# A hybrid layer in one kernel: a pool shared by two projection stages with early loads, gate rows on GpSimd's queue, and x normalised in pairs of tiles

## The chip, the core and the metric

The kernel runs on one core of a Trainium2 chip. The metric is the device time of one execution in microseconds, and a kernel's time is the median of its runs.

## What is computed

One layer of a streaming encoder on x, 2048 tokens by 1024 channels in float32. The stream is normalised, and one projection w_in makes the columns of four mixers: S5 (a diagonal complex state space model), RWKV-7, stick-breaking attention and an mLSTM with a matrix memory. Their outputs, 256 channels each, are concatenated and projected; then follows a gated feed-forward with a causal convolution. Of the reference, the parts that the change touches:

```python
def layer_norm(x, g, b):
    xf = x.astype(jnp.float32)
    mu = jnp.mean(xf, -1, keepdims=True)
    var = jnp.mean(jnp.square(xf - mu), -1, keepdims=True)
    return ((xf - mu) * lax.rsqrt(var + LN_EPS) * g + b).astype(x.dtype)
...
    b = jnp.cumsum(chunks(jax.nn.log_sigmoid(fg)), axis=-1)
    b_last = b[..., -1]
    g = b_last[..., None] - b + ig
    m_loc = jnp.max(g, -1)
...
        m_new = jnp.maximum(bl + m_st, ml)
        s_old = jnp.exp(bl + m_st - m_new)
        s_new = jnp.exp(ml - m_new)
```

The first function is the input normalisation. The rest is the mLSTM's gate arithmetic: the input gates ig and forget gates fg, four rows (heads) by 2048 tokens, give decays and a running maximum for every token.

## The kernel before

Every large product is made in three matmuls: both factors are split into a high and a low part (`wch`, `wcl` for weights, `hTh`, `hTl` for tokens), and high by high, low by high and high by low are summed. A projection of 128 columns over a block of 512 tokens is 8 pieces of the inner dimension times 3, 24 matmuls of 128x512. The instructions of each engine run in the order in which a scheduler puts them from the program; each engine, and each queue of transfers, is in order. A tile pool gives out its buffers again when the last use of a tile is over, and a pool that is opened later may get the memory of a closed one, and then waits for that one's last uses.

The stages, by the time at which TensorE works at them: P, the projections of S5 and RWKV (0 to about 363 us), with S5's set-up and its four blocks between them; Q, the projections of the attention and the mLSTM, begins behind S5's last block and then fills gaps in R (RWKV, to about 1045 us); S (attention) with X (mLSTM) to about 1425 us; the output projection O to about 1605; the feed-forward U and D to the end.

*Stage P* (`phase_p`) has four blocks of 512 tokens. `layer_in(tb)` loads four tiles of x (128 tokens each), takes mean and variance on VectorE (`bn_stats`, `bn_aggr`), the reciprocal root on GpSimd (`rsqrt`), -mean*rs and the normalised tile on VectorE (lines 290 and 291). TensorE transposes the tiles (line 298), VectorE makes u = p*g+b (line 300), ScalarE rounds u to the high part (line 301), and VectorE and GpSimd in turn subtract it to get the low part (line 302). Both parts go to the scratch tensor `hT_d`, from which stage Q reads its tokens again. `layer_in` of the next block is called at the end of a block.

*Stage Q* (`phase_q`) opens its own pools after those of P are closed. It loads a block's tokens in eight transfers, then its weights, and splits them (`load_w`: ScalarE rounds, GpSimd subtracts). Its small constants come by GpSimd's queue.

*Stage X* (`phase_x`) starts with the gate rows: r_f and r_ig are loaded as 64 rows of 128 from `gt_d`, which Q wrote; r_lf, the log of the sigmoid, goes to `ml_lf_d`; then four steps, one for each block of 512 tokens, load two rows of gates, scan them with VectorE (`mrow`, line 666) and store the result (`ml_m_d`, `ml_p_d`). The scans' results are read back as r_mr and r_mp, from which come the rows that are stored to `ml_rowd` and loaded again as `mb` and `wib`. All these transfers are issued by SP's queue, in which the loads of attention stand too: `kst` (keys), `qdh` and `qdl` (queries in two parts), `v` and `sb_dv` (values). In the attention, TensorE makes scores (`a`, from `kst` and `qdh`), ScalarE turns them into `sb_stay`, VectorE scans them (`af`, line 507), TensorE transposes the scan (`b`) and multiplies it with the values (`c`).

## Time and profile before

| | before |
|---|---|
| median of 3 runs | 2933.1 us (2932.53 to 2935.2) |
| the profiled execution, its own time | 2929.18 us |
| span in the profile | 2927.5 us |
| mean granted clock of TensorE | 0.967 of full |
| TensorE (PE) busy | 2744.1 us, 94% |
| VectorE (DVE) busy | 1944.7 us, 66% |
| ScalarE (ACT) busy | 1249.4 us, 43% |
| GpSimd (POOL) busy | 753.8 us, 26% |

A profile follows one execution. Its times count from the start of the span. PE is TensorE's matmuls, PEld its loading of weights, SP an engine that only issues transfers; a q behind a name is that engine's queue. A row of a timeline gives start, duration, engine, line, operation, what is written and what is read, the tile's size and, in brackets, how long the engine was idle before and whose work ended that. "Full clock" is 2.4 GHz, and 0.50 of it 1.2 GHz.

### The profile page before, as it was taken

To read this page: it belongs to the slowest core of one execution; us is meant where nothing else is said; L and a number is where in the kernel's file an instruction comes from. 1 tells how busy PE (TensorE), PEld (TensorE's weight loads), DVE (VectorE), ACT (ScalarE), POOL (GpSimd) and SP (SyncE) were. 2 spreads that over 40 slices of the span, in tenths; PEclk is the share of its full clock that TensorE was granted. 3 is DMA by queue.
4 is the path that set the end of the run, shared out by engine and by line. 5 is a ranking of instruction groups with operands and counts; after the bars stand their busy time and mean duration, and the time that the engine had idled before them with its cause. 6 is when DMAs were issued, how large, how long until landed. Compare 5 with 4: busy or idle time off the path is not lost. (4 is left out here: it accounts for less than half of the span.)

```text
span 2927.5 us, 42242 instructions
## 1 busy us (share of the span) xinstructions
PE 2744.1 (94%) x15515; PEld 2168.4 (74%) x15515; DVE 1944.7 (66%) x3109; ACT 1249.4 (43%) x2103; POOL 753.8 (26%) x800
## 2 busy tenths in 40 slices
...
GB/s 182 130 207 218 155 188 136 171 122 174 117 138 121 58 176 158 133 54 69 224 241 204 208 154 160 151 166 260 229 197 198 195 194 195 246 265 189 198 160 123
DMA packets 495775, 502.51 MB, mean 172 GB/s; under 512 B 105088, under 2 KB 383488, under 8 KB 492752
## 3 DMA queue, kind: packets, MB, share of 16 engines
...
q14 instruction: 85, 0.70, 0.1%
q10 hardware_dynamic: 1744, 0.14, 0.0%
...
## 5 line engine op out<-in xcount | busy, mean ns | idle before, releaser
L143 PE MATMUL u_ps<-bh,wh 128*128 128x512 f32 x1232 | 482.7, 392 | 5.1 <-ACT hr L189 1.8
L144 PE MATMUL u_ps<-bl,wh 128*128 128x512 f32 x1232 | 481.9, 391 | 0.3 <-DVE bl L1483 0.3
L145 PE MATMUL u_ps<-bh,wl 128*128 128x512 f32 x1232 | 480.3, 390 | 0.0
L1513 ACT CAST wh<-wr 128x512 fp32r<-128x512 f32 x308 | 191.1, 622 | 412.6 <-PE u_ps L144 326.0
L135 POOL TENSOR_TENSOR wcl<-wraw,wch 128x512 fp32r<-128x512 f32 (+1 forms) x152 | 249.1, 1649 | 448.2 <-ACT wch L132 419.7
L1514 DVE TENSOR_TENSOR wl<-wr,wh 128x512 fp32r<-128x512 f32 x308 | 210.9, 687 | 164.1 <-ACT wh L1513 163.8
L143 PEld LDWEIGHTS u_ps<-bh,wh 128*128 128x128 f32 x1232 | 231.5, 188 | 58.4 <-ACT g L1615 2.1
L145 PEld LDWEIGHTS u_ps<-bh,wl 128*128 128x128 f32 x1232 | 231.5, 188 | 50.3
L144 PEld LDWEIGHTS u_ps<-bl,wh 128*128 128x128 f32 x1232 | 231.7, 188 | 48.7 <-DVE bl L1483 0.6
L1571 POOL DMA_DIRECT2D ad_d<-cv x132 | 95.5, 726 | 639.0 <-DVE cv L1557 607.7
L132 ACT CAST wch<-wraw 128x512 fp32r<-128x512 f32 (+1 forms) x152 | 110.2, 731 | 263.8 <-PE m L144 146.7
L143 PE MATMUL m<-hT,wch 128*128 128x512 f32 x448 | 189.2, 424 | 3.7 <-ACT wch L132 2.8
L145 PE MATMUL m<-hT,wcl 128*128 128x512 f32 x448 | 184.9, 413 | 2.6 <-POOL wcl L135 2.6
L144 PE MATMUL m<-hT,wch 128*128 128x512 f32 x448 | 184.2, 412 | 0.0
L106 DVE TENSOR_TENSOR da<-da 128x1024 fp32r<-128x1024 f32 (+1 forms) x84 | 104.8, 1280 | 65.1 <-ACT da L103 64.9
L103 ACT CAST da<-da 128x1024 fp32r<-128x1024 f32 (+1 forms) x84 | 79.5, 976 | 149.5 <-DMA da<-ad_d 149.0
L507 DVE TENSOR_TENSOR_SCAN af<-sb_stay,af,sb_zero 128x513 f32<-128x513 f32 x96 | 120.4, 1274 | 28.8 <-ACT sb_stay L502 26.7
L144 PE MATMUL m<-hTl,wch 128*128 128x512 f32 x320 | 130.6, 408 | 7.5 <-POOL hTl L302 6.6
L143 PE MATMUL m<-hTh,wch 128*128 128x512 f32 x320 | 127.4, 404 | 6.9 <-DVE rw_halo L336 6.9
L145 PE MATMUL m<-hTh,wcl 128*128 128x512 f32 x320 | 127.3, 398 | 0.0
L502 ACT ACTIVATE sb_stay<-a 128x512 f32<-128x512 f32 (+3 forms) x160 | 86.0, 539 | 91.7 <-PE a L498 43.1
L1553 DVE SCALAR_TENSOR_TENSOR cv<-u,ffn_cw,cv 128x1024 f32<-128x1024 f32 x88 | 112.7, 1281 | 15.8 <-ACT cv L1551 15.7
...
## 6 DMA issues: line engine op xcount, KB each, us to landing
...
ad_d<-S POOLq DMA_DIRECT2D x176, 128.0 KB, 3.8
...
ad_d<-cv POOLq DMA_DIRECT2D x132, 128.0 KB, 2.8
```

Of the source, the lines that this page charges most:

```text
L106: nc.vector.tensor_tensor(lo, src, r32(hi), op=ALU.subtract)
L132: nc.scalar.copy(hi[:, kk, cs], raw)
L135: (lo_eng or nc.vector).tensor_tensor(lo[:, kk, cs], raw, r32(hi[:, kk, cs]), op=ALU.subtract)
L143: nc.tensor.matmul(ps, lh, rh, start=start and i == 0, stop=False, **kw)
L144: nc.tensor.matmul(ps, lh, rl, start=False, stop=False, **kw)
L145: nc.tensor.matmul(ps, ll, rh, start=False, stop=i == n - 1, **kw)
L502: nc.scalar.activation(r[:, ns], lgn, AF.Sigmoid, scale=-1.0)
L507: nc.vector.tensor_tensor_scan(af[:, back], r[:, back], zero.to_broadcast([128, n + 1]), p["af"][:, TB - p["n"]:TB - p["n"] + 1] if p else ...
L1513: nc.scalar.copy(h, r)
L1514: V(l, r, r32(h), op=ALU.subtract)
L1553: STT(cv, u[:, d:d + 1024], cw[:, f, d:d + 1], cv, op0=ALU.mult, op1=ALU.add)
L1571: nc.gpsimd.dma_start(K_.ad_d[i - 1, fb, c, :, j, :].rearrange("p (n c) -> p n c", c=128), t[:, 2 * c:2 * c + 2, :])
```

## The change

It does four things.

1. A new pool, `early`, holds the tiles of x, u, and the token blocks of every other block, and Q's token blocks and weights use the same buffers. It stays open from the start of P to the end of Q. `hT_d` becomes one tensor for each block, written in eight transfers.
2. `phase_q` is started inside P's last block, ahead of the third of its six last RWKV projections (`QAT`): it then loads its first token block and its first two weights. Its constants live in the kernel's constant pool and are loaded by SP's queue.
3. In `layer_in`, the reciprocal root is taken for two tiles at once; -mean*rs is a `tensor_scalar`; the normalised tile is made by ScalarE from block 1 on, and for the second tile of each pair in block 0; u is made by ScalarE from block 1 on, and the low parts there all by VectorE. x is requested ahead of the norm's gain and bias.
4. The 22 transfers of the gate rows go from SP's to GpSimd's queue.

```diff
...
         rs = pool.tile([128, 1], F32, tag="ln_rs", name="ln_rs")
         self.rsqrt(pool, rs, mv[:, 1:2], LN_EPS)
         nm = pool.tile([128, 1], F32, tag="ln_nm", name="ln_nm")
-        nc.vector.scalar_tensor_tensor(nm, mv[:, 0:1], -1.0, rs, op0=ALU.mult, op1=ALU.mult)
+        nc.vector.tensor_scalar(nm, mv[:, 0:1], rs, -1.0, op0=ALU.mult, op1=ALU.mult)
         nc.scalar.activation(t, t, AF.Identity, scale=rs, bias=nm)
...
     return cv
-def phase_p(K_, st, st5):
+def phase_p(K_, st, st5, early, ahead):
...
             q(nc).dma_start(t, src.rearrange("(f p) -> p f", p=128))
             return t
-        def layer_in(tb):
+        def xrows(tb):
             xs = []
             for i in range(4):
...
+                x = early.tile([128, D], F32, tag="x", bufs=4, name="x")
+                nc.sync.dma_start(x, a["x"][0, (tb * 4 + i) * 128:(tb * 4 + i) * 128 + 128, :])
                 xs.append(x)
-            hi = w.tile([128, KD, TB], F32R, tag="hTh", name="hTh")
-            lo = w.tile([128, KD, TB], F32R, tag="hTl", name="hTl")
+            return xs
+        def layer_in(tb, xs):
+            for j in range(0, 4, 2):
+                mv = w.tile([128, 2, 2], F32, tag="ln_mv", name="ln_mv")
+                for i in range(2):
+                    st = w.tile([128, 2, 6], F32, tag="ln_st", bufs=4, name="ln_st")
+                    for q in range(2):
+                        nc.vector.bn_stats(st[:, q, :], xs[j + i][:, q * 512:(q + 1) * 512])
+                    nc.vector.bn_aggr(mv[:, i], st)
+                ti = tb * 4 + j
+                K_.rsqrt(w, K_.lnst[:, ti:ti + 2, 1], mv[:, :, 1], LN_EPS)
+                for i in range(2):
+                    x, nm, rs = xs[j + i], K_.lnst[:, ti + i, 0:1], K_.lnst[:, ti + i, 1:2]
+                    TS(nm, mv[:, i, 0:1], rs, -1.0, op0=ALU.mult, op1=ALU.mult)
+                    if tb or i:
+                        nc.scalar.activation(x, x, AF.Identity, scale=rs, bias=nm)
+                    else:
+                        TS(x, x, mv[:, i, 0:1], rs, op0=ALU.subtract, op1=ALU.mult)
+            hs = [token_block((early, w)[tb % 2]) for _ in range(4)]
+            hT = [(h[:, k, :], l[:, k, :]) for h, l in hs for k in range(2)]
             for k in range(KD):
                 p = K_.psum("a", 2) if tb == 0 else K_.psum("c", 1)
                 for i in range(4):
                     nc.tensor.transpose(p[:, i * 128:(i + 1) * 128], xs[i][:, k * 128:(k + 1) * 128], K_.ident)
-                u = w.tile([128, TB], F32, tag="u", name="u")
-                TS(u, p, g[:, k:k + 1], b[:, k:k + 1], op0=ALU.mult, op1=ALU.add)
-                nc.scalar.copy(hi[:, k, :], u)
-                last = (nc.gpsimd if k % 2 else nc.vector).tensor_tensor(lo[:, k, :], u, r32(hi[:, k, :]),
-                                                                         op=ALU.subtract)
+                u = early.tile([128, TB], F32, tag="u", bufs=2, name="u")
+                if tb:
+                    nc.scalar.activation(u, p, AF.Identity, scale=g[:, k:k + 1], bias=b[:, k:k + 1])
+                else:
+                    TS(u, p, g[:, k:k + 1], b[:, k:k + 1], op0=ALU.mult, op1=ALU.add)
+                nc.scalar.copy(hT[k][0], u)
+                last = (nc.gpsimd if tb == 0 and k % 2 else nc.vector).tensor_tensor(hT[k][1], u, r32(hT[k][0]), op=ALU.subtract)
             K_.hold = last.ins
-            nc.sync.dma_start(K_.hT_d[tb, 0], r32(hi))
-            nc.sync.dma_start(K_.hT_d[tb, 1], r32(lo))
-            return [(hi[:, k, :], lo[:, k, :]) for k in range(KD)]
+            for q, t in enumerate(hs):
+                for i in range(2):
+                    nc.sync.dma_start(K_.hT_d[tb][i][:, 2 * q:2 * q + 2, :], r32(t[i]))
+            return hT
+        xs = xrows(0)
         g, b = chan("ln_in_g", a["ln_in_g"], KD, P1Q), chan("ln_in_b", a["ln_in_b"], KD, P1Q)
-        hT = layer_in(0)
+        hT = layer_in(0, xs)
         mu = chan("rw_mu", a["rw_mu"][0], 8, P2Q)
...
             nc.scalar.activation(xg, xg, AF.Sigmoid)
             nc.sync.dma_start(K_.rz_d[tb, 10], xg)
             for s in (2, 0, 4, 3, 1, 5):
+                if s == QAT and tb == K_.ntb - 1:
+                    ahead()
                 nc.sync.dma_start(K_.rz_d[tb, s], mixed(s))
-            hT = layer_in(tb + 1) if tb + 1 < K_.ntb else None
+            hT = layer_in(tb + 1, xrows(tb + 1)) if tb + 1 < K_.ntb else None
             if tb == FCB:
...
+def token_block(pool):
+    return [pool.tile([128, 2, TB], F32R, tag=n, bufs=4, name=n) for n in ("hTh", "hTl")]
+def phase_q(K_, st, early):
     tc, nc, a = K_.tc, K_.nc, K_.a
     w_in = a["w_in"][0]
     STT = nc.vector.scalar_tensor_tensor
-    c = st.enter_context(tc.tile_pool(name="qc", bufs=1, reuse_waits="tile", side="right"))
+    c = K_.const
+    def tokens(tb):
+        hT = []
+        for q in range(4):
+            hq = token_block(early)
+            for i in range(2):
+                HTQ(nc).dma_start(r32(hq[i]), K_.hT_d[tb][i][:, 2 * q:2 * q + 2, :])
+            hT += [(hq[0][:, k, :], hq[1][:, k, :]) for k in range(2)]
+        return hT
+    def weights(c0):
+        hi, lo = (early.tile([128, KD, 128], F32R, tag="x", bufs=4, name=n) for n in ("wch", "wcl"))
+        for k in range(0, KD, 4):
+            raw = early.tile([128, 4, 128], F32, tag="u", bufs=2, name="raw")
+            nc.sync.dma_start(raw, w_in.rearrange("(k p) n -> p k n", p=128)[:, k:k + 4, c0:c0 + 128])
+            nc.scalar.copy(hi[:, k:k + 4], raw)
+            nc.gpsimd.tensor_tensor(lo[:, k:k + 4], raw, r32(hi[:, k:k + 4]), op=ALU.subtract)
+        return hi, lo
+    hT, first = tokens(0), [weights(OFF_MLQ + i * 128) for i in range(2)]
+    yield
     w = st.enter_context(tc.tile_pool(name="qw", bufs=2, reuse_waits="tile", side="right"))
     cw = c.tile([128, 4, 4], F32, name="ml_cw")
     for j in range(4):
-        nc.gpsimd.dma_start(cw[:, :, j], a["ml_conv_w"][0, j].rearrange("(f p) -> p f", p=128))
+        nc.sync.dma_start(cw[:, :, j], a["ml_conv_w"][0, j].rearrange("(f p) -> p f", p=128))
...
     for tb in range(K_.ntb):
         tcs = slice(tb * TB, (tb + 1) * TB)
-        hT = []
-        for q in range(4):
-            hq = [w.tile([128, 2, TB], F32R, tag=f"hT{i}", bufs=4, name=f"hT{i}") for i in range(2)]
-            for i in range(2):
-                HTQ(nc).dma_start(r32(hq[i]), K_.hT_d[tb, i][:, 2 * q:2 * q + 2, :])
-            hT += [(hq[0][:, k, :], hq[1][:, k, :]) for k in range(2)]
+        if tb:
+            hT = tokens(tb)
         def cm(c0):
-            wt = load_w(K_, w, w_in, c0, 128, "wc", 2, rawpool=w, rtag="raw", rbufs=QRB, kpiece=4, eng=QENG, lo_eng=nc.gpsimd)
+            wt = first.pop(0) if first else weights(c0)
             p = K_.psum("mm", 3)
             proj_cm(K_, wt, hT, p)
             return p
...
     row = lambda n: c.tile([NG, L], F32, name="r_" + n)
     ig, f, lf, na, bb, gg, mr = (row(n) for n in ("ig", "f", "lf", "na", "b", "g", "mr"))
     mp, ml = c.tile([NG, 1], F32, name="r_mp"), c.tile([NG, 1], F32, name="r_ml")
-    nc.sync.dma_start(f, hc(K_.gt_d[4:8]))
-    nc.sync.dma_start(ig, hc(K_.gt_d[0:4]))
+    nc.gpsimd.dma_start(f, hc(K_.gt_d[4:8]))
+    nc.gpsimd.dma_start(ig, hc(K_.gt_d[0:4]))
     nc.vector.scalar_tensor_tensor(na, f, -1.0, f, op0=ALU.mult, op1=ALU.min)
...
     for tb in range(K_.ntb):
         cs = slice(tb * TB, (tb + 1) * TB)
         l4, i4 = (w.tile([128, TB], F32, tag=f"qw{n}", bufs=1, name="gates")[0:4] for n in range(2))
-        nc.sync.dma_start(l4, lf_d[:, cs])
-        nc.sync.dma_start(i4, K_.gt_d[0:4, cs])
+        nc.gpsimd.dma_start(l4, lf_d[:, cs])
+        nc.gpsimd.dma_start(i4, K_.gt_d[0:4, cs])
         if tb:
             nc.vector.tensor_copy(mrow[:, 0:1], mrow[:, TB:TB + 1])
         nc.vector.tensor_tensor_scan(mrow[:, 1:], l4, i4, mrow[:, 0:1], op0=ALU.add, op1=ALU.max)
-        nc.sync.dma_start(m_d[:, cs], mrow[:, 1:])
-        nc.sync.dma_start(p_d[:, tb * NCH:(tb + 1) * NCH], mrow[:, 0:TB:L])
-    nc.sync.dma_start(mr, hc(m_d))
-    nc.sync.dma_start(mp, p_d.rearrange("h c -> (h c)").unsqueeze(1))
+        nc.gpsimd.dma_start(m_d[:, cs], mrow[:, 1:])
+        nc.gpsimd.dma_start(p_d[:, tb * NCH:(tb + 1) * NCH], mrow[:, 0:TB:L])
+    nc.gpsimd.dma_start(mr, hc(m_d))
+    nc.gpsimd.dma_start(mp, p_d.rearrange("h c -> (h c)").unsqueeze(1))
...
     dr = lambda name, *sh: k.dram.tile(list(sh), F32, name=name)
     k.z5_d = dr("z5_d", k.ntb, 2, 128, S5J, S5N)
     k.y5_d = dr("y5_d", k.ntb, 128, 8, S5N)
-    k.hT_d = dr("hT_d", k.ntb, 2, 128, KD, TB)
+    k.hT_d = [dr(f"hT_d{tb}", 2, 128, KD, TB) for tb in range(k.ntb)]
...
-    left, right = ExitStack(), ExitStack()
+    left, right, right_p = ExitStack(), ExitStack(), ExitStack()
+    early = right.enter_context(tc.tile_pool(name="px", bufs=1, reuse_waits="tile", side="right"))
+    q = phase_q(k, right, early)
     s5 = none
     if "P" in parts:
-        for tb, _ in enumerate(phase_p(k, right, left)):
+        for tb, _ in enumerate(phase_p(k, right_p, left, early, lambda: next(q))):
             if tb == 0:
                 s5 = ahead(s5_main(k, left), S5HP)
             for _ in range(S5_IN_P[tb]):
                 next(s5, None)
-        right.close()
-    q = phase_q(k, right) if "Q" in parts else none
+        right_p.close()
...
 HTQ, ZQ, YQ, CQ = SY, SY, SY, SY
-QRB, QENG = 2, "act"
+QAT = 4
...
```

The lines of the changed program are numbered anew; the rows below carry the new numbers for the changed order.

On TensorE, at the seam between P and Q, the rows before are the last products of S5's fourth block (`b`, from the scans' result `Sx`) and the start of Q's first projection (`m1_3014`):

```order
L1379 MATMUL b_3201<-Sx1_2880,s5_CI_365 128x128
L1377 MATMUL b_3201<-U_2874,s5_MT_366 128x128
L1379 MATMUL b_3201<-Sx0_2879,s5_CR_364 128x128
L1379 MATMUL b_3201<-Sx1_2880,s5_CI_365 128x128
L143 MATMUL m1_3014<-hT0_2988,wch_3004 128x512
L144 MATMUL m1_3014<-hT1_2989,wch_3004 128x512
```


Of the change, at the same place. First the end of Q's second projection (`m2_3081`; the first, `m1_3043`, stands in front of it) and the first products of S5's fourth block (`b_3158`), with Q's third projection (`m0_3182`) between them:

```order
L144 MATMUL m2_3081<-hTl_2702,wch_2715 128x512
L145 MATMUL m2_3081<-hTh_2701,wcl_2716 128x512
L1416 MATMUL b_3158<-U_2932,s5_MT_376 128x128
L1418 MATMUL b_3158<-Sx0_2937,s5_CR_374 128x128
L1418 MATMUL b_3158<-Sx1_2938,s5_CI_375 128x128
L1416 MATMUL b_3158<-U_2932,s5_MT_376 128x128
L143 MATMUL m0_3182<-hTh_2689,wch_3172 128x512
L1418 MATMUL b_3158<-Sx0_2937,s5_CR_374 128x128
L144 MATMUL m0_3182<-hTl_2690,wch_3172 128x512
```


and, some 30 rows further, the end of the third projection, the first of the other products of that block (`b_3220`) and the matmuls of S5's output gate (`m1_3244`):

```order
L143 MATMUL m0_3182<-hTh_2701,wch_3172 128x512
L144 MATMUL m0_3182<-hTl_2702,wch_3172 128x512
L1418 MATMUL b_3220<-Sx0_2937,s5_CR_374 128x128
L145 MATMUL m0_3182<-hTh_2701,wcl_3173 128x512
L1434 MATMUL m1_3244<-yc_2992,s5_wglu_1115 128x512 x2
L1418 MATMUL b_3220<-Sx1_2938,s5_CI_375 128x128
L1416 MATMUL b_3220<-U_2932,s5_MT_376 128x128
```


Q's first projection came behind all products of S5's fourth block; now two projections come ahead of them and the third among them.

On SP's queue, in the middle of the attention, before: the last two steps of the gate rows, with the attention's loads between them.

```order
L667 DMA ml_m_d<-mrow 4x512
L668 DMA ml_p_d<-mrow 4x4x1
L662 DMA gates<-ml_lf_d 4x512
L663 DMA gates<-gt_d 4x512
L562 DMA qdh<-sk_d 64x2x512
L563 DMA qdl<-sk_d 64x2x512
L667 DMA ml_m_d<-mrow 4x512
L668 DMA ml_p_d<-mrow 4x4x1
L567 DMA v<-sv_d 128x2x256
L567 DMA sb_dv<-sv_d 128x2x256
L669 DMA r_mr<-ml_m_d 64x128
L670 DMA r_mp<-ml_p_d 64x1
```


Of the change, at the same place of the attention; `mb` and `wib` are the first loads that need the finished gate rows.

```order
L600 DMA kst<-sk_d 64x4x512
L601 DMA qdh<-sk_d 64x2x512
L602 DMA qdl<-sk_d 64x2x512
L600 DMA kst<-sk_d 64x4x512
L601 DMA qdh<-sk_d 64x2x512
L602 DMA qdl<-sk_d 64x2x512
L606 DMA v<-sv_d 128x2x256
L606 DMA sb_dv<-sv_d 128x2x256
L734 DMA mb<-ml_rowd 128x4x512
L740 DMA wib<-ml_rowd 64x2x512 x2
L606 DMA v<-sv_d 128x2x256
L606 DMA sb_dv<-sv_d 128x2x256
```


The loads of `kst`, `qdh`, `qdl` and the first values now stand ahead of everything that has to do with gate rows; the second pair of values stands behind `mb` and `wib`.

On GpSimd, of the change, the head of the gate rows (`ml_mask` is a constant of the mLSTM; its memory is that of one of Q's tiles, and it waits for the last matmuls of Q's last projection):

```order
L668 MEMSET ml_mask 128x128
L685 DMA r_f<-gt_d 64x128
L669 AFFINE_SELECT ml_mask<-ml_mask 128x128
L686 DMA r_ig<-gt_d 64x128
L691 DMA ml_lf_d<-r_lf 64x128
L701 DMA gates<-ml_lf_d 4x512
L702 DMA gates<-gt_d 4x512
L706 DMA ml_m_d<-mrow 4x512
L707 DMA ml_p_d<-mrow 4x4x1
L701 DMA gates<-ml_lf_d 4x512
```


None of these transfers stood on GpSimd before; all that stood there around this place was the two instructions on `ml_mask`.

## Rows read from the trace of the kernel before

**Rows 1.** The page, part 1: busy us (share) x instructions of each engine.

```profile
PE 2744.1 (94%) x15515; PEld 2168.4 (74%) x15515; DVE 1944.7 (66%) x3109; ACT 1249.4 (43%) x2103; POOL 753.8 (26%) x800
```

**Rows 2.** Timeline of PE, 0 to 60 us: start us, us, instruction [idle before <-releaser].

```profile
22.78 0.69 PE L298 MATMUL a<-ident,x 128*128 128x128 f32 x2 [5.55 <-DVE x L291]
...
58.33 0.47 PE L298 MATMUL c<-ident,x 128*128 128x128 f32 x1 [10.41 <-DVE x L291]
```

**Rows 3.** Waits of PE: waited for, us in total, times, longest us.

```profile
PE m L143 <- DVE rw_halo L336: 6.9, 1, 6.9
```

**Rows 4.** Timeline of PE, 363 to 400 us.

```profile
380.97 0.80 PE L1379 MATMUL b<-Sx,s_CR 128*128 128x128 f32 x2 [6.78 <-DVE Sx L1361]
...
387.31 0.77 PE L143 MATMUL m<-hT,wch 128*128 128x512 f32 x1
...
393.11 0.39 PE L145 MATMUL m<-hT,wcl 128*128 128x512 f32 x1
397.10 1.95 PE L1395 MATMUL m<-yc,s_wglu 128*128 128x512 f32 x4 [3.60 <-DVE ml_halo L259]
```

**Rows 5.** Timeline of PE, 1090 to 1150 us.

```profile
1136.02 0.66 PE L497 MATMUL a<-kst,qdh 128*128 128x128 f32 x2 [11.37 <-DMA qdh<-sk_d]
1137.28 0.44 PE L498 MATMUL a<-kst,qdl 128*128 128x128 f32 x1 [0.60 <-DMA qdl<-sk_d]
...
1142.41 0.36 PE L681 MATMUL m<-ident,r_ig 64*128 64x64 f32 x1 [0.98 <-ACT r_ig L675]
```

**Rows 6.** Stretches: length, busy (x) of five engines, PEclk, DMA share, GB/s.

```profile
40.00:60.00 20.00, 9.45 (x51) 7.07 (x49) 19.52 (x54) 6.07 (x15) 10.14 (x7) 0.76 0.60 227
360.00:380.00 20.00, 13.66 (x87) 10.93 (x85) 19.42 (x43) 7.84 (x10) 1.75 (x4) 0.95 0.63 181
380.00:400.00 20.00, 13.87 (x52) 10.49 (x52) 7.83 (x16) 5.62 (x9) 3.19 (x3) 0.79 0.63 202
1130.00:1145.00 15.00, 7.40 (x34) 5.37 (x34) 5.77 (x11) 4.87 (x10) 0.00 (x0) 0.50 0.59 151
```

**Rows 7.** Timeline of DVE, 5 to 30 us.

```profile
17.60 2.29 DVE L290 SCALAR_TENSOR_TENSOR lnst<-ln_mv,lnst 128x1 f32<-128x1 f32 x1 [1.00 <-POOL lnst L78]
19.81 2.91 DVE L291 TENSOR_SCALAR x<-x,ln_mv,lnst 128x1024 f32<-128x1024 f32 x1
```

**Rows 8.** Lines 291 to 302: count, ns min/median/max, first and last start, forms.

```profile
L291 DVE TENSOR_SCALAR x<-x,ln_mv,lnst x16: 799/806/2908, 10.2 to 272.4; 128x1024 f32<-128x1024 f32 x16
...
L300 DVE TENSOR_SCALAR u<-c,ln_in_g,ln_in_b x24: 780/800/811, 124.6 to 302.0; 128x512 f32<-128x512 f32 x24
...
L301 ACT CAST hTh<-u x32: 608/620/624, 24.1 to 302.8; 128x512 fp32r<-128x512 f32 x32
...
L302 DVE TENSOR_TENSOR hTl<-u,hTh x16: 661/679/693, 25.2 to 301.4; 128x512 fp32r<-128x512 f32 x16
```

**Rows 9.** Timeline of SP's queue, 1090 to 1145 us.

```profile
1131.52 0.58 SPq L562 DMA_DIRECT2D qdh<-sk_d  x1
```

**Rows 10.** Line 1571, issues on GpSimd's queue: count, ns min/median/max.

```profile
L1571 POOL DMA_DIRECT2D ad_d<-S x176: 540/552/575, 1653.0 to 2470.0; - x176
```

**Rows 11.** Transfers: queue, count, KB each, median us from issue to landing.

```profile
ml_cw<-in_ml_conv_w_dram POOLq DMA_DIRECT2D x4, 2.0 KB, 2.5
...
sv_d<-zr POOLq DMA_DIRECT2D x1, 1.0 KB, 7.3
```

**Rows 12.** Timeline of DVE, 1123 to 1146 us.

```profile
1123.10 2.43 DVE L507 TENSOR_TENSOR_SCAN af<-sb_stay,af,sb_zero 128x513 f32<-128x513 f32 x2
```

**Rows 13.** Timeline of ACT, around 1062 and 1100 us.

```profile
1062.87 0.70 ACT L502 ACTIVATE sb_stay<-a 128x128 f32<-128x128 f32 x2 [9.68 <-PE a L500]
...
1099.42 1.28 ACT L649 ACT_TABLE_LOAD   x1
```

29 lines of the change are left out of this document (8 added, 21 removed).

## The prediction

> **What bounds the kernel now.** I read the page's busy shares first. TensorE is busy 2744.1 of 2927.5 us [rows 1], so the whole kernel holds about 183 us that any rearrangement could win, and the change leaves every matrix product in the program. I then split the span by stretches and read the waits of TensorE, to see where those 183 us lie and which of them the edits touch. From 1430 us on (output projection and feed-forward) the order of the instructions stays as it is, but for the kind of one small VectorE instruction per tile, so everything that can change lies before about 1250 us. Four places there matter:
>
> - the start, where TensorE waits for normalised tiles of x and then 10.41 us for the first tile of block 1 [rows 2];
> - the normalisation of blocks 1 to 3 inside the projections, where the longest wait is 6.9 us for VectorE [rows 3];
> - the seam between projections and the loop of Q (attention and mLSTM projections), where TensorE waits 6.78 us for S5's scan and 3.60 us more after Q's first projection [rows 4];
> - the middle of the attention, where it waits 11.37 us for a query tile [rows 5].
>
> In the stretches one sees what an idle stretch costs beside itself: the granted clock is 0.79 of full in 380 to 400 us and 0.50, which is 1.2 of 2.4 GHz, in 1130 to 1145 us, after the two long waits [rows 6].
>
> **A. The start: 5 us.** Each of block 0's tiles is normalised by VectorE. The fourth is late because two small VectorE instructions took 2.29 and 2.91 us [rows 7], where the shortest of the second kind took 0.80 [rows 8]. By the neighbouring rows some 2.2 and 2.1 us of that were a stall; at that time GpSimd ran the splitting of a weight. The change replaces the first instruction by a plain tensor_scalar and gives tiles 1 and 3 to ScalarE, which takes 2 x 0.81 us [rows 8] from VectorE: 4.3 + 1.6 = 5.9 us less in front of the fourth tile, against a ScalarE pass of some 1 us in its place. The 10.41 us [rows 2] go in another way: the transposes of block 1's first tile no longer stand ahead of S5's set-up on TensorE. But VectorE is busy 19.52 of 20 us in 40 to 60 us [rows 6] with that set-up, and it is what TensorE meets next. So only what VectorE saves counts. I take 5; the ends are 0 (set-up keeps the end where it is) and 10 (the whole wait goes).
>
> **B. Blocks 1 to 3: 4 us.** VectorE gives up 12 passes over x (0.81 us) and 24 passes u = p*g+b (0.80), and takes 12 subtractions that GpSimd did (0.68) [rows 8]: 9.7 + 19.2 - 8.2 = 20.7 us less. ScalarE gets 24 passes over 128x512, for which the nearest row is its 0.62 us cast [rows 8], and 12 of twice the length: some 15 + 15 = 30 us more, in a stretch where it is less than half busy. GpSimd's 12 slow subtractions go. TensorE gains only what waits for VectorE at the seams; the one large such wait is 6.9 us [rows 3]. Against it stands a new chain: u and its cast are both ScalarE's now, 0.62 + 0.62 = 1.24 us for each of 8 pieces, 10 us per block, where VectorE and ScalarE overlapped before. TensorE has 4 transposes and 3 matmuls per piece to cover this, which is about as long. I take 4; ends -6 and 10.
>
> **C. The seam: 9 us.** Today Q's first projection starts at 387.31 us, its last matmul at 393.11 [rows 4], behind all of S5's last block. The changed order puts two projections of Q ahead of that block's products and a third among them; their tokens and weights come from the shared pool, so they needn't wait for the projections' pools to close. By the two rows one projection, 24 matmuls, is 5.8 us from its first start to its last, the first ones at a lower clock. Two of them, some 11 us, now lie where TensorE waited. I don't count the third, nor the 3.60 us: the output gate of S5's last block needs VectorE's scan, a store and a load, so TensorE will again stand there, around 390 to 397 us, having done two projections more. Some small products are left behind that wait: 11 less 2 is 9. Ends: 5 (one projection) and 13 (with the clock of [rows 6] restored).
>
> **D. The gate rows: 11 us.** In the SP queue the query load stands at 1131.52 us behind m_d and p_d [rows 9], which wait for VectorE's scans; it lands and TensorE resumes at 1136.02, then waits 0.60 and 0.98 more [rows 5], at half clock: 7.40 us of work took twice what it needs, 3.7 too much [rows 6]. Moved to GpSimd's queue, the gate transfers leave SP free, and the loads stand ahead of them: 11.37 + 0.60 + 0.98 + 3.7 = 16.6 us removed. What comes instead is on VectorE. A step of the row scan needs four issues on GpSimd's queue and one landing. The trace's nearest issue is 0.55 us [rows 10], its shortest landing of small transfers 2.5 [rows 11]: 4.7 us a step, and 6.1 for the last, which needs two landings. The changed VectorE order gives as cover between the four scans, at 1.2 us for each full attention scan [rows 12] and less for the short ones: 4.8, 2.0, 3.7, and 5.4 before the last. Uncovered: 0 + 2.7 + 1.0 + 0.7 = 4.4 us, and attention scans, thus TensorE, stand queued behind. At the head of the attention the chain r_f to r_g now runs before the first attention scan, and TensorE needs r_g after two score pairs. ScalarE is idle for 9.68 us there and can load its two tables (1.28 each [rows 13]) then; r_f's transfer can't start before the last projection ends. I put 1 us on it, so D is 16.6 - 4.4 - 1 = 11. Ends: -32 (next part) and 18.
>
> The Trainium skill speaks against this move ("SBUF — State Buffer", the "DVE blocks DMA" trap): the descriptors of a transfer from GpSimd's queue are written by GpSimd, which is locked out while VectorE runs a two-port operation, and the page advises SP's or ScalarE's queue. The 176 issues of one kind on this queue took 540 to 575 ns [rows 10], though VectorE is busy two thirds of the time [rows 1]; nothing in that row is stretched, so the sum goes by the row.
>
> **Sum.** 5 + 4 + 9 + 11 = 29 us off the profiled execution, 2929.2 us, gives 2900. That execution lies 3.9 us under the median of the runs shown, 2933.1; off the median it is 2904, and that is what I predict. Other parts I cost at nothing: Q's constants by SP (hidden during blocks 0 and 1), hT stored in eight pieces for two (SP has room, and nobody waits for the stores), one DRAM tensor per block (it only removes a dependency).
>
> **Rivals.** *The lock on descriptors decides.* If each gate issue waits for one attention scan (1.2 us [rows 12]), a step is 9.5 us, uncovered are 4.7 + 7.5 + 5.8 and 3 at the end, 21 us: D is 16.6 - 21 = -4, the total 14 off, 2919. This is the page's rule as a mechanism; the even issues speak against, the two stalled VectorE instructions of [rows 7] for some sharing between the engines. Chance 0.14.
>
> *Slower: the gate transfers land late.* Another small transfer of GpSimd's queue took 7.3 us [rows 11]. At that, steps are 9.5 and the last 15.7 us: 4.7 + 7.5 + 5.8 + 10.3 = 28 uncovered, 7 at the head, 8 at rowd, where SP's loads of the mLSTM queue behind GpSimd, and 5 at half clock: 48 against 16.6 removed, so -32. With 18 from A to C that is 2947. It decides above a landing of about 6 us. Chance 0.08.
>
> *VectorE's S5 work holds the projections.* It was busy 19.42 of 20 us at 360 to 380 [rows 6]. If its set-up and scans set the ends whatever comes earlier, A is 0, B 2, C 7: 20 off, 2913. Chance 0.16.
>
> *More than counted*: A whole, C with its clock, attention without a stall: 10 + 6 + 12 + 15 = 43 off, 2890. For it speaks that the removed idle stretches at the seam and in the attention were followed by a lower clock [rows 6]. Chance 0.12.
>
> **Numbers.** The forecast (2895 to 2911) has 0.50. The range 2884 to 2927 leaves out the slower case and the tails. About 0.2% (6 us) can be told from no change; faster takes all cases but the slower one and the edge of the lock case: 0.88, same 0.04, slower 0.08.
>
> **What would show it.** A: the fourth tile done near 17 us, first projection some 5 us earlier. B: no wait over 5 us for VectorE in 90 to 320 us. C: Q's matmuls ahead of S5's last products, one wait of 5 to 9 us at the output gate. D: no wait of TensorE for the query tile; scans of the gate rows 4 to 7 us apart; waits of VectorE for the gates' transfers of about 4 us in all. Wrong if those waits exceed 15 us, or if TensorE waits over 10 us in a block's normalisation for ScalarE.

## The result and the profile after

The changed kernel takes **2903.06 us** (median of 4 runs, 2896.11 to 2914.04); the kernel before took 2934.15 on the same chip (2932.53 to 2935.35). The ratio is 0.9895, with a 95% interval from 0.9862 to 0.9928: 31 us faster, where 29 were forecast. The profiled execution, though, is the slowest of the four, 2914.04 us with a span of 2912.3, only 15 us below the one of before. So the total hides a good deal, and the way to read it is by stretches.

Page, part 1, of the changed kernel: busy us (share of the span) x instructions.

```profile
PE 2759.4 (95%) x15515; PEld 2174.2 (75%) x15515; DVE 1920.4 (66%) x3083; ACT 1283.1 (44%) x2140; POOL 734.0 (25%) x787
```

Against [rows 1], TensorE has the same 15,515 instructions and is busy 15.3 us longer. Nothing in the change makes a product larger, so this is a first hint of something the prediction did not have.

For the stretches I use the start of SP's instruction at the end of each: the last rz_d store of a block of P, gt_d of Q's block 0, the seventh and the sixteenth store yT_d<-y (end of the R loop and of the attention), the last store bm_d<-hr (end of the output projection), the last load of wr (end of U, the up projection) and the last load of da (end of the down projection). Of the changed kernel these are, among others:

```profile
340.73 0.32 SPq L379 DMA_DIRECT2D rz_d<-ev  x1
...
416.91 0.29 SPq L463 DMA_DIRECT2D gt_d<-ev  x1
...
1242.33 0.34 SPq L767 DMA_DIRECT2D yT_d<-y  x1
...
1583.89 0.71 SPq L192 DMA_DIRECT2D bm_d<-hr  x1
...
2383.80 0.38 SPq L1530 DMA_DIRECT2D wr<-in_ffn_w_up_dram  x1
```

| end of | before, us | after, us | difference | added in the stretch |
|---|---|---|---|---|
| P, block 0 | 128.1 | 119.2 | -8.9 | -8.9 (A) |
| P, block 3 | 365.5 | 340.7 | -24.7 | -15.8 (B) |
| Q, block 0 | 451.2 | 416.9 | -34.3 | -9.6 (C) |
| R loop | 1012.6 | 980.6 | -32.0 | +2.3 |
| attention | 1269.2 | 1242.3 | -26.9 | +5.1 (D) |
| output projection | 1612.6 | 1583.9 | -28.8 | -1.9 |
| U | 2403.0 | 2383.8 | -19.2 | +9.6 |
| down projection | 2888.6 | 2874.1 | -14.5 | +4.7 |

The prediction's four parts gave 25 where 9 were forecast (A and B), 9.6 where 9 (C), and minus 5 where 11 (D). Then 14 us are lost again in the feed-forward, where the order of TensorE's instructions is as it was.

**The start.** The fourth tile of block 0 is transposed at 16.44 us, not at 22.78, and the first product starts at 19.43, not at 25.78. But the next ones wait (TensorE, 20 to 40 us), and the twenty-fourth product starts at 37.59 us, where it started at 35.67 before:

```profile
24.14 0.50 PE L144 MATMUL m<-hTl,wch 128*128 128x512 f32 x1 [3.08 <-DVE hTl L316]
...
29.77 1.11 PE L309 MATMUL a<-ident,x 128*128 128x128 f32 x4 [3.79 <-DVE u L314]
```

So nothing of this start reaches the end of block 0. What does is that the wait of 10.41 us [rows 2] is gone: the transposes of block 1 now begin at 114.72 us, with no wait.

**Blocks 1 to 3 of P.** Waits of TensorE from 120 to 310 us (waited for, us in total, times, longest us), before and then after:

```profile
PE m L144 <- POOL hTl L302: 6.2, 9, 1.4
PE c L298 <- DVE ln_mv L287: 5.2, 1, 5.2
PE c L298 <- DVE u L300: 2.8, 3, 2.1
PE m L352 <- DVE ev L335: 0.8, 1, 0.8
PE m L144 <- DVE hTl L302: 0.6, 1, 0.6
```

```profile
PE m L367 <- DVE ev L350: 2.4, 3, 0.8
PE m L144 <- DVE hTl L316: 0.3, 1, 0.3
```

Fourteen waits for the normalisation, 14.8 us, became one of 0.3 us; 2.4 us for ev stand where 0.8 stood. The wait of [rows 3] is not among them: it lies at 111 us, in block 0, where 4.45 us of it are left.

**The seam.** From the end of P to the end of Q's block 0 (340.7 to 416.9 us by the table) one wait of TensorE begins and ends, 2.32 us, where the same stretch before (365.5 to 451.2) had nine, 15.7 us in all, the largest of them in [rows 4]. A second one, of 5.40 us, ends at 418.34, at the first products of R, which wait for ScalarE; before, the products at that place waited 0.38 us:

```profile
369.30 0.49 PE L1418 MATMUL b<-Sx,s_CR 128*128 128x128 f32 x2 [2.32 <-DVE Sx L1400]
...
418.34 1.86 PE L977 MATMUL a<-rw_blk,sq 128*128 128x2 f32 x8 [5.40 <-ACT sq L974]
```

The gain stands all the same: these products started at 453.67 us before, 35.3 us later. Every kernel below that has the new order at the seam has this wait, 4.96 to 6.51 us.

In the first three stretches of [rows 6] TensorE is now busy 17.37, 17.68 and 20.00 of 20 us:

```profile
40.00:60.00 20.00, 17.37 (x69) 10.32 (x67) 19.55 (x67) 10.61 (x21) 8.58 (x6) 0.89 0.61 182
360.00:380.00 20.00, 17.68 (x84) 12.94 (x83) 17.50 (x34) 10.98 (x14) 5.26 (x4) 0.91 0.44 128
380.00:400.00 20.00, 20.00 (x82) 13.77 (x81) 10.35 (x25) 6.77 (x11) 6.42 (x5) 1.00 0.54 161
```

**The attention.** The wait of 11.37 us for the query tile [rows 5] is gone. In its place, waits of TensorE from 1000 to 1290 us:

```profile
PE b L554 <- DVE af L546: 12.9, 6, 4.0
PE m L720 <- DVE r_g L694: 5.2, 1, 5.2
PE m L832 <- DVE cst L815: 4.1, 1, 4.1
PE m L720 <- ACT r_ig L714: 3.0, 1, 3.0
PE a L536 <- DMA qdh<-sk_d: 2.9, 1, 2.9
```

VectorE is late in most of them, and its timeline tells why (start us, us, instruction, idle before and releaser):

```profile
1032.61 0.28 DVE L687 SCALAR_TENSOR_TENSOR r_na<-r_f 64x128 f32<-64x128 f32 x1 [9.15 <-DMA r_f<-gt_d]
...
1078.17 0.14 DVE L704 COPY mrow<-mrow 4x1 f32<-4x1 f32 x1 [2.93 <-DMA ml_p_d<-mrow]
...
1090.17 0.14 DVE L704 COPY mrow<-mrow 4x1 f32<-4x1 f32 x1 [7.63 <-DMA ml_p_d<-mrow]
...
1098.58 1.27 DVE L705 TENSOR_TENSOR_SCAN mrow<-gates,mrow 4x512 f32<-4x512 f32 x1 [2.43 <-DMA gates<-gt_d]
```

It stands idle 9.15 us for the first row and 2.93 + 7.63 us for stores of 0.1 KB that must land before mrow may be written again, with the attention's scans queued behind. GpSimd was not held up in the issues themselves:

```profile
1024.65 0.21 POOL L668 MEMSET ml_mask<- 128x128 f32 x1 [4.34 <-PE m L144]
1024.80 0.79 POOL L685 DMA_DIRECT2D r_f<-gt_d  x1
...
1092.86 0.50 POOL L706 DMA_DIRECT2D ml_m_d<-mrow  x1 [9.34 <-DVE mrow L705]
1093.40 0.64 POOL L707 DMA_DIRECT2D ml_p_d<-mrow  x1
```

The transfers are what takes long. Queue, count, KB each, median us from issue to landing:

```profile
gates<-ml_lf_d POOLq DMA_DIRECT2D x4, 8.0 KB, 4.9
gates<-gt_d POOLq DMA_DIRECT2D x4, 8.0 KB, 5.0
...
r_f<-gt_d POOLq DMA_DIRECT2D x1, 32.0 KB, 7.8
ml_lf_d<-r_lf POOLq DMA_DIRECT2D x1, 32.0 KB, 5.7
r_mr<-ml_m_d POOLq DMA_DIRECT2D x1, 32.0 KB, 2.6
```

From 1075 to 1090 us the DMA engines are full (share 1.07, the column before GB/s), from 1090 on they are not (0.17), and eight of the ten gate transfers that are issued later land in 1.7 to 2.7 us:

```profile
1075.00:1090.00 15.00, 11.77 (x113) 9.42 (x109) 4.40 (x6) 6.83 (x15) 2.15 (x4) 1.00 1.07 255
1090.00:1105.00 15.00, 11.39 (x57) 8.66 (x57) 11.75 (x14) 5.79 (x13) 4.35 (x8) 0.66 0.17 33
```

The other two, the loads of gates at 1094 us, took 4.3 and 4.0 us with the DMA engines nearly idle. So the load on them is not all of it; what held these two is open.

### The profile page after: what moved, and what is told of

The parts are those of the page before. It is cut to its first block, busy times and chain, and to the rows that moved or that the text cites. A ratio compares the mean times of both kernels' runs of the same rounds, so it can differ in the third digit from the quotient of the medians.

```text
span 2912.3 us, 42246 instructions
## 1 busy us (share of the span) xinstructions
PE 2759.4 (95%) x15515; PEld 2174.2 (75%) x15515; DVE 1920.4 (66%) x3083; ACT 1283.1 (44%) x2140; POOL 734.0 (25%) x787
## 4 chain that ended last, share of the span: by engine, by line
PE 47%; issue 7%; DMA 5%; DVE 4%; ACT 2%; POOL 1%; SPq 0%; POOLq 0%; DVEq 0%; ACTq 0%
PE u_ps L144 9%; PE u_ps L143 9%; PE u_ps L145 9%; PE m L143 3%; PE m L145 3%; PE m L144 3%; PE c L573 1%; DMA da<-ad_d 1%; PE b L554 1%; DVE db L106 1%; PE a L536 1%; DVE af L546 1%; PE m L850 1%; PE b L143 1%; PE b L145 1%
## 5 line engine op out<-in xcount | busy, mean ns | idle before, releaser
L143 PE MATMUL m<-hTh,wch 128*128 128x512 f32 x768 | 321.5, 421 | 7.5 <-DVE rw_halo L351 4.5
L144 PE MATMUL m<-hTl,wch 128*128 128x512 f32 x768 | 316.0, 413 | 3.5 <-DVE hTl L316 3.4
L145 PE MATMUL m<-hTh,wcl 128*128 128x512 f32 x768 | 313.8, 409 | 1.3 <-POOL wcl L414 1.3
L414 POOL TENSOR_TENSOR wcl<-raw,wch 128x512 fp32r<-128x512 f32 x112 | 152.0, 1369 | 334.7 <-ACT wch L413 317.8
L143 PEld LDWEIGHTS m<-hTh,wch 128*128 128x128 f32 x768 | 147.7, 193 | 46.6 <-issue 10.0
L144 PEld LDWEIGHTS m<-hTl,wch 128*128 128x128 f32 x768 | 147.0, 192 | 38.7 <-DVE hTl L316 6.6
L145 PEld LDWEIGHTS m<-hTh,wcl 128*128 128x128 f32 x768 | 147.6, 192 | 31.9 <-POOL wcl L414 2.2
L413 ACT CAST wch<-raw 128x512 fp32r<-128x512 f32 x112 | 68.5, 617 | 145.3 <-PE m L144 100.8
L135 POOL TENSOR_TENSOR wcl<-wraw,wch 128x1024 fp32r<-128x1024 f32 x40 | 96.4, 2415 | 143.5 <-ACT wch L132 140.3
L1592 DVE SCALAR_TENSOR_TENSOR cv<-u,ffn_cw,cv 128x1024 f32<-128x1024 f32 x88 | 112.7, 1281 | 15.8 <-ACT cv L1590 15.7
```

What stands on the lines that cost most here:

```text
L135: (lo_eng or nc.vector).tensor_tensor(lo[:, kk, cs], raw, r32(hi[:, kk, cs]), op=ALU.subtract)
L143: nc.tensor.matmul(ps, lh, rh, start=start and i == 0, stop=False, **kw)
L144: nc.tensor.matmul(ps, lh, rl, start=False, stop=False, **kw)
L145: nc.tensor.matmul(ps, ll, rh, start=False, stop=i == n - 1, **kw)
L414: nc.gpsimd.tensor_tensor(lo[:, k:k + 4], raw, r32(hi[:, k:k + 4]), op=ALU.subtract)
L1592: STT(cv, u[:, d:d + 1024], cw[:, f, d:d + 1], cv, op0=ALU.mult, op1=ALU.add)
```

## The experiments

Each kernel was timed beside the kernel before on its chip. "End of" and "stretch" mean those of the table. From profile to profile, block 0 ended 3.6 to 9.7 us earlier than before, blocks 1 to 3 gained 15.8 to 17.3 and the seam 9.6 to 11.3 (over the seven kernels that leave the instructions of both as in the change). The kernel before moves too: in gate_only and pad_before, where the instructions of these stretches are its own, block 0 ended 1.8 and 2.7 us earlier than in its profile, blocks 1 to 3 differed by at most 0.4 and the seam took 0.5 and 2.7 us more. So the blocks can be read from one profile, the seam to some 2 us; the start and the total can't, to better than several us. The attention differed from before by -0.4 to 3.3 us in the three other kernels with the gate rows on SP (gate_sp, align_sp, pad_before) and by 2.0 to 7.6 in the seven with them on GpSimd's queue as in the change.

**1. The gate rows back on SP (gate_sp).** All `nc.gpsimd.dma_start` of the gate rows become `nc.sync.dma_start`; the rest is the changed kernel.

```diff
-    nc.gpsimd.dma_start(f, hc(K_.gt_d[4:8]))
+    nc.sync.dma_start(f, hc(K_.gt_d[4:8]))
...
-        nc.gpsimd.dma_start(l4, lf_d[:, cs])
+        nc.sync.dma_start(l4, lf_d[:, cs])
```

> The changed kernel with the 22 gate transfers back on SP's queue. My theory after the two traces: the start, the blocks and the seam give some 34 us, and the move of the gate rows gives nothing (the attention loses 5 us in the trace, because the small transfers land after 5 to 8 us while bulk loads fill the DMA engines, and VectorE stands in order behind them). Then this kernel is 0 to 8 us faster than the changed one: about 2896 to 2903, with the wait of some 11 us for the query tile back and the wait for r_f at the head of the attention gone. Rival, the prediction's own part D: the move gives 11 us; then this kernel takes about 2914.

2899.49 us, ratio 0.9879 [0.9852, 0.9905]: not slower than the changed kernel. The wait for the query tile is back (waits of TensorE, 1000 to 1290 us),

```profile
PE a L536 <- DMA qdh<-sk_d: 14.3, 2, 11.3
PE m L832 <- DVE cst L815: 4.0, 2, 3.2
```

and the attention takes 0.4 us less than in the kernel before, where the changed kernel takes 5.1 more. The move removes a wait and pays for it with others. This run also shows where the start's spread comes from: in P its code is that of the changed kernel, but TensorE waits once more for VectorE, and block 0 gains 7.3 us in place of 8.9 (TensorE, 50 to 60 us):

```profile
55.02 2.07 PE L367 MATMUL m<-ev,rw_wa 64*128 64x512 f32 x2 [4.16 <-DVE ev L350]
```

**2. Only the gate rows moved (gate_only).** The kernel before, with the gate rows' 23 transfers on GpSimd's queue (23 by the trace; the list of the change says 22).

```diff
-    nc.sync.dma_start(f, hc(K_.gt_d[4:8]))
+    nc.gpsimd.dma_start(f, hc(K_.gt_d[4:8]))
```

> The kernel before with the gate transfers on GpSimd's queue and nothing else. My theory: between no change and 6 us slower than before (2934 to 2940), with VectorE waiting for the small store p_d and for gates as in the changed kernel. Prediction's part D: 11 us faster, 2923. Rival of the lock on descriptors: issues on GpSimd's queue stretched well over 0.6 us.

2942.63 us, ratio 1.0019 [1.0000, 1.0038]. The attention takes 6.7 us more than before, and VectorE's scans are late again:

```profile
PE b L515 <- DVE af L507: 12.7, 5, 7.2
```

Alone or with the rest, part D gains nothing. U took 790.2 us here, 790.3 in the kernel before, 799.9 in the changed one: the loss in the feed-forward doesn't come from the gate rows.

**3. The old normalisation (norm_back).** The changed kernel with tile by tile normalisation on VectorE, u on VectorE, every second subtraction on GpSimd.

```diff
-                    if tb or i:
-                        nc.scalar.activation(x, x, AF.Identity, scale=rs, bias=nm)
...
+                TS(x, x, mv[:, 0:1], rs, op0=ALU.subtract, op1=ALU.mult)
```

> The changed kernel with x normalised as before (one tile at a time, x and u by VectorE, low parts half by GpSimd); the shared pool, early loads and gate rows stay. My theory: the 25 us that the trace shows gained by the end of block 3 come mostly from this part (A and B): 15 to 22 us slower than the changed kernel, 2918 to 2925. Rival: they come from the earlier requests of x and from the changed order at block 1 (transposes after S5's set-up), which stay here: then under 6 us slower, 2909.

2918.31 us, ratio 0.9937 [0.9912, 0.9962]. Blocks 1 to 3 gain 1.6 us in place of 15.8, and the old waits stand there (120 to 310 us):

```profile
PE m L144 <- POOL hTl L309: 5.5, 8, 1.2
PE c L304 <- DVE x L298: 5.0, 1, 5.0
PE m L144 <- DVE hTl L309: 2.1, 5, 0.7
```

The seam still gains 9.9, block 0 still 5.4 by the profile of before, 2.7 and 3.6 by those of pad_before and gate_only. So B is worth 14 us here, and much of A's gain is not the normalisation's.

**4. Q's first loads late (late_q).** Q's first tokens and weights are loaded after P's pools close; they still lie in the shared pool.

```diff
-                if s == QAT and tb == K_.ntb - 1:
-                    ahead()
...
         right_p.close()
+        next(q)
```

> The changed kernel with stage Q started only after stage P has closed its own pools (no early loads); the shared pool stays. My theory: the seam's 9 us go: 2912. Rival: the shared pool and the separate scratch tensors alone let Q's first loads go early enough: 0 to 3 us slower, 2903 to 2906.

2912.32 us, ratio 0.9914 [0.9892, 0.9936]. The seam gains 8.3 us, against 9.6 to 11.3, and its one wait is 3.0 us for VectorE's Sx. By this one profile the early issue is worth 1 to 3 of the 9.6. The rest comes with what this run leaves in place: the shared pool, one scratch tensor for each block, Q's constants by SP. That it is the shared pool, whose tiles don't wait for P's pools to close, is likely but was not separated. The totals' ratios overlap.

**5. Two addresses (align).** Across the profiles of the kernels that leave addresses alone, U takes 790.2 or 790.3 us with Q's constants in their own pool and 798.6 to 802.1 with them in the constants pool, which that makes 992 bytes longer, so that every tile on the left lies elsewhere. This kernel makes it 960 bytes and puts 32 into P's constants.

```diff
+        c.tile([128, 8], F32, name="pad")
...
-    zr = c.tile([128, 2], F32, name="zr")
+    zb = c.tile([128, 8], F32, name="zr")
+    zr, bif = zb[:, 0:2], zb[0:8, 2:3]
-    bif = c.tile([8, 1], F32, name="ml_bif")
```

> The changed kernel with two addresses moved and nothing else: zr and the gate bias share one 32-byte tile, so that the constants pool has grown by 960 bytes and not 992 against the kernel before, and a 32-byte dummy tile in P's constants; every operand pair of a projection then starts at the same address modulo 64 bytes. Theory M (a matmul whose two operands lie at different 32-byte halves of a 64-byte line is spaced more widely): the spacing of one matmul in U goes from 230.3 back to 228.0 ns and in D from 234.3 to 233.3, in P's blocks 0 and 2 from about 231 to 227; 3,696 matmuls of U by 2.3 ns are 8.5 us, D 2, P 3 to 4: about 2889 us, at least 8 below the changed kernel. Rival N (the spacing comes from something else that the change brought, the shared pool's releases or the traffic): spacings as in the changed kernel and a time within 4 us of 2903.

2896.23 us, ratio 0.9839 [0.9802, 0.9877]. P's block 2 shows the effect in clean rows. Forty consecutive products of the changed kernel, first and last (start us, us):

```profile
227.80 0.40 PE L143 MATMUL m<-hTh,wch 128*128 128x512 f32 x1
...
236.90 0.40 PE L143 MATMUL m<-hTh,wch 128*128 128x512 f32 x1
```

and forty of this kernel:

```profile
227.74 0.39 PE L145 MATMUL m<-hTh,wcl 128*128 128x512 f32 x1
...
236.58 0.39 PE L145 MATMUL m<-hTh,wcl 128*128 128x512 f32 x1
```

39 spacings are 9.10 us, 233.3 ns each, against 8.84 us, 226.7 ns, both at a granted clock of 1.00 (2.4 GHz). The changed kernel shows both by itself: the tokens of its blocks 0 and 2 lie in the shared pool, where operands and next weights start 32 bytes apart modulo 64, and its products are spaced by 233.3 ns there; those of blocks 1 and 3 lie in P's own pool, start equal modulo 64, and are spaced by 227.4 and 227.3. In U the mean went from 230.3 to 228.9 ns only, and U took 795.2 us: half of the loss came back. D's went from 234.3 to 232.8, under the 233.3 of before, which was not expected.

**6. An unused tile in the kernel before (pad_before).** 32 bytes at the end of the constants pool; no instruction changes.

```diff
     k.lnst = k.const.tile([128, seq // 128, 2], F32, name="lnst")
+    k.const.tile([128, 8], F32, name="pad")
```

> The kernel before with one unused 32-byte tile more in the constants pool, which moves every pool on the left by 32 bytes and changes no instruction. Theory M: the spacing of a matmul in U goes from 228.0 to about 230.3 ns, in D from 233.3 to 234.3, P's stays at 227; 8 to 11 us slower than before, about 2943 to 2946. Rival N: no spacing changes, and the time stays within 3 us of before.

2940.44 us, ratio 1.0002 [0.9980, 1.0023]; the kernel before ran from 2919.44 to 2953.4 us on that chip, so the total is no support; its interval ends at 6.8 us more, below the 8 to 11 expected. U does show it: it takes 798.7 us, 8.4 more. One product has 229.4 ns there, less than the 230.3 expected, so 3,696 x 1.4 = 5.2 us of the 8.4 are spacing; D's spacing stayed at 233.3, a miss. Sorted by the addresses that the build gives to the tiles, the records of U show, for spacings under 260 ns:

```
kernel       left pools   pairs whose starts differ mod 64   equal pairs   U
             moved by     count      mean spacing            mean spacing
before            0 B         0         -                     228.0 ns     790.3 us
pad_before       32 B      1135      233.5 ns                 227.6 ns     798.7 us
changed         992 B      1135      233.5 ns                 228.9 ns     799.9 us
align           960 B         0         -                     228.9 ns     795.2 us
px_const          0 B         0         -                     228.0 ns     791.8 us
```

A pair is the moving operand of a product and the weights of the next one (loaded while it runs). Where one starts at 0 and the other at 32 modulo 64 bytes, the spacing in U is 4.6 to 5.8 ns larger, in a kernel whose instructions did not change too. D does not follow this: all its pairs are equal in the kernel before and all differ in pad_before, and the spacing is 233.3 ns in both.

**7. Gate rows without round trips (both).** The loads of all four blocks go ahead into tiles of their own, two mrow rows are taken in turn, and the attention's pools open in the other order, so that r_f's transfer doesn't stand behind the memset that waited for Q's last product.

```diff
+    mrows = [mrow[0:4, 0:1 + TB], mrow[0:4, 1 + TB:]]
...
+        nc.gpsimd.dma_start(gates[tb][0], lf_d[:, cs])
+        nc.gpsimd.dma_start(gates[tb][1], K_.gt_d[0:4, cs])
...
+        mrow = mrows[tb % 2]
```

> The changed kernel with the gate rows' loads for all four token blocks issued ahead into tiles of their own and two mrow rows taken in turn, so that no scan waits for a store to land, and with the pools of the attention opened in the other order, so that the first load of the gate rows no longer waits for Q's last projection. Theory T (VectorE's scans wait in order for small transfers that land late, and TensorE's first chunks wait for VectorE): the waits of VectorE at the scans (2.4 to 7.6 us each) go, the first rows are there some 5 us earlier, and the end comes 5 to 10 us earlier than in the changed kernel: 2893 to 2898. Rival R (the attention is held by the loads themselves and by the evictions behind them, whichever row they wait for): within 3 us of the changed kernel, other waits at the same place.

2902.97 us, ratio 0.9862 [0.9833, 0.9892]. In the trace the waits shrink as wanted: VectorE's for ml_p_d from 10.6 to 2.7 us, TensorE's for af from 12.9 to 5.3.

```profile
DVE r_na L687 <- DMA r_f<-gt_d: 10.4, 1, 10.4
...
DVE r_f L719 <- DMA r_mr<-ml_m_d: 3.2, 1, 3.2
DVE mrow L712 <- DMA ml_p_d<-mrow: 2.7, 2, 1.5
```

The attention takes 2.7 us less than before where the changed kernel takes 5.1 more, 8 us between them. The total doesn't show it beyond its spread, and the wait for r_f, issued 8.6 us earlier, stays (10.4 us): opening the pools in the other order only moved it.

**8. Both edits (align_both).** The edits of 5 and 7 together.

> The two edits together (addresses and gate rows). If M and T both hold, the gains add: about 2880 to 2885. If M holds alone 2889, if T alone 2893 to 2898, if neither 2903.

2891.26 us, ratio 0.9831 [0.9802, 0.9860], on one chip with 5 and 7: 11.7 us under the gate edits alone (which ran from 2891.44 to 2905.06, this from 2886.94 to 2898.43) and 5.0 under the addresses alone. The addresses' gain shows in the total; the 5.0 of the gate edits lie within the spread of experiment 5 (2882.09 to 2904.04), though the trace has them. The sum is short of 2880 to 2885. The attention takes 0.3 us less than before, U 795.0.

**9. GpSimd's subtractions back (pool_lo).**

```diff
-(nc.gpsimd if tb == 0 and k % 2 else nc.vector)
+(nc.gpsimd if k % 2 else nc.vector)
```

> The changed kernel with one thing of the normalisation undone: in blocks 1 to 3 every second subtraction that makes the low part of a token tile is GpSimd's again, as in the kernel before. Theory S (the gain of blocks 1 to 3 is a sum of many short waits, among them nine for GpSimd's subtraction, 6.2 us in 120 to 310 us): those waits come back, and the end of P lies 5 to 9 us later than in the changed kernel (351.2 us there), of the 16 us that blocks 1 to 3 gained. Rival V (what counts is VectorE's load): VectorE has 8 us less to do, and the end of P is the same or earlier.

What such a subtraction takes on GpSimd is read from the kernel before, groups by line from 138 to 216 us (busy us, mean ns | idle before); on VectorE it is 679 ns [rows 8]:

```profile
L302 POOL TENSOR_TENSOR hTl<-u,hTh 128x512 fp32r<-128x512 f32 x4 | 5.8, 1442 | 13.3 <-ACT hTh L301 13.3
```

2911.22 us, ratio 0.9886 [0.9845, 0.9928]. Blocks 1 to 3 gain 6.0 us in place of 15.8: the twelve subtractions alone cost 9.8, of which some 7 stand as waits of TensorE, and P ends 8.7 us later. Waits, 120 to 310 us:

```profile
PE m L144 <- POOL hTl L316: 4.0, 6, 1.0
PE m L144 <- DVE hTl L316: 3.5, 2, 2.6
```

The load of VectorE, less by 8 us here, did not matter.

**10. The passes back on VectorE (dve_u).** Pairs and subtractions as changed, the passes over x and u on VectorE.

```diff
-                    if tb or i:
+                    if tb == 0 and i:
...
-                if tb:
+                if False:
```

> The changed kernel with the passes over x and the passes u = p*g+b of blocks 1 to 3 on VectorE again (pairs of tiles and the subtractions as in the change). Theory S: VectorE has 29 us more in three blocks and 8 more than before the change, so it holds the pieces up: end of P 8 to 16 us later than in the changed kernel, with waits for VectorE at the transposes of 5 us or more. Rival A (the pairs and the subtractions made the gain, and the passes were hidden): within 3 us of 351.2.

2916.30 us, ratio 0.9909 [0.9883, 0.9935]. P ends 10.0 us later, 4.4 of them by the end of block 0, whose spread is as large; blocks 1 to 3 gain 10.3 us, 5.5 less than in the changed kernel. The longest wait is 2.6 us, not the 5 expected: the passes count for about a third, the subtractions for two thirds. That split is rough: of the 5.5 us only 2.5 stand as waits, and the granted clock was 0.74 from 140 to 160 us, where the changed kernel has 1.00.

**11. Addresses, and the gate rows on SP (align_sp).** The edits of 5 and 1 together.

> The changed kernel with the two addresses moved and the gate rows' transfers back on SP: the change without its part D and without the spacing. If the move to GpSimd's queue is worth nothing, as the run with SP's queue alone showed, this is level with the run that only moved the addresses, 0.984 of the kernel before, or up to 5 us faster; if the move gains what was predicted, 11, it is slower by that.

2898.09 us, ratio 0.9852 [0.9831, 0.9874]: level with experiment 5, as for a move worth nothing. The attention takes 2.4 us more than before, against 7.5 with the same addresses and GpSimd's queue.

**12. Q's constants in the shared pool (px_const).** As experiment 8, with one line more: nothing on the left lies elsewhere than before.

```diff
-    c = K_.const
+    c = early
```

> The kernel with addresses and gate rows edited, and Q's constants in the shared pool instead of the constants pool: nothing on the left side lies elsewhere than in the kernel before, and P's and Q's operands still share a start modulo 64 bytes. U took 790.3 us in the kernel before, 799.9 in the changed kernel and 795.0 where all pairs are equal modulo 64 but lie 960 bytes further. Theory M2 (the rest is a matter of the addresses too): U takes 790 to 791 us again with 228.0 ns a matmul, some 5 us less than in the run with both edits; D's matmul has 233.3 ns as in the kernel before. Rival (what is left in U comes from what else the change brought): U stays at 795. The total is 2885 to 2889 by M2, against 2891 for the run with both edits and constants where the change puts them.

2893.86 us, ratio 0.9836 [0.9808, 0.9865]; level with experiment 8 in the total, not better as expected. But U takes 791.8 us, a product 228.0 ns in U and 233.3 in D, as in the kernel before. The same 680 us of U, 1700 to 2380, in the changed kernel, and then here; the count of TensorE's instructions is in the third column:

```profile
1700.00:2380.00 680.00, 678.42 (x2944) 551.98 (x2943) 473.29 (x676) 313.85 (x521) 151.10 (x244) 1.00 0.60 191
```

```profile
1700.00:2380.00 680.00, 677.78 (x2972) 557.29 (x2971) 477.38 (x684) 317.17 (x526) 154.16 (x248) 1.00 0.61 194
```

28 products more, at the same clock and under the same transfers. So 8.1 of the 9.6 us that U had lost go with the addresses; the 1.5 left are less than the 3.5 us by which U differed between kernels with the change's addresses. The total doesn't show it; the R loop takes 8.3 us more than before here, at a granted clock of 0.94 (0.96 before), and no run explains that.

## Why the prediction was right, and where it was not

The time, the sign and the range held, the time in good part by luck: the blocks gained 12 us more than forecast, the gate rows 16 less, and 14 were lost in the feed-forward, for which nothing had been set. The profiled execution is 15 us off, half of the 29; only the median is 31.

- **A, start: 5 forecast, 8.9 in the profile, 3.6 to 9.7 over the repeats.** Right within its ends, but not by the way that was counted. The step that failed is "So only what VectorE saves counts". VectorE's shorter chain did bring the first product some 6 us forward, as forecast, but 24 products later nothing of it was left, because the pieces then waited for VectorE (3.08 and 3.79 us). What won is what had been set aside: the transposes of block 1 no longer stand ahead of S5's set-up, and the wait of 10.41 us is gone. norm_back, with the old instructions on VectorE, still gains. The reason for setting it aside, that the set-up on VectorE holds the end, holds in part: seven of the kernels with the change's start wait 4.2 to 6.0 us for VectorE at 55 to 57 us and gain 3.6 to 7.3; the changed kernel, px_const and pool_lo have no such wait and gain 8.9 to 10.1.
- **B, blocks 1 to 3: 4 forecast, ends -6 to 10; 15.8 measured, outside.** The step that failed is "TensorE gains only what waits for VectorE at the seams; the one large such wait is 6.9 us". The row behind the 6.9 us lies in block 0; in blocks 1 to 3 the longest wait was 5.2 us, for the mean and variance of a tile (ln_mv). Nine waits of at most 1.4 us for GpSimd's subtractions were left out; giving these back alone costs 9.8 us (pool_lo), giving the passes back 5.5 (dve_u). "GpSimd's 12 slow subtractions go" stood there without a price. They took 1442 ns each against VectorE's 679 [rows 8]. The feared chain on ScalarE shows no wait in these blocks.
- **C, seam: 9 forecast, 9.6 measured.** Right in size. Loading early is worth only 1 to 3 of it (late_q); most comes with the shared pool and what else late_q leaves in place. The wait of 5 to 9 us at S5's output gate, for which room had been left, did not come there; 2.32 us for S5's scan remain, and 5.40 us at the first products of R. How much of that is owed to the lighter VectorE was not separated; with the old normalisation the seam gained as much (9.9).
- **D, gate rows: 11 forecast, -5.1 measured,** within its ends, but of the wrong sign. The removed wait was read rightly. The loss is small against the spread, but the seven kernels with this move lie 5.4 us above before in the mean, the three others with SP's queue 1.7. The step that failed is the landing: "its shortest landing of small transfers 2.5". Under full DMA engines the gate transfers took 4.7 to 8.2 us, and the ml_p_d stores held mrow for 10.6 us. VectorE waited 23 us for gate transfers at r_f and at the scans, more than the 15 us that the prediction itself had called a sign of being wrong, and the scans came 7 to 12 us apart. This is the rival "the gate transfers land late" in mechanism, at a fraction of its price: it said above 6 us and -32, and the loss was 5. That prefetched rows bring 8 us back shows it (both). The "lock on descriptors" as the rival had it, each issue held for an attention scan, is not what happened: the issues took 0.50 to 0.79 us, also while scans ran, and the stores at 1092.86 and 1093.40 us landed within 1.8 us though VectorE was scanning. The 9.34 us GpSimd waited were for VectorE's scan, in program order. The Trainium skill's rule ("SBUF — State Buffer", the "DVE blocks DMA" trap) speaks of two-port operations of VectorE; no issue in this trace is held by a scan, and which of VectorE's operations here are of that kind no run shows.
- **"From 1430 us on (output projection and feed-forward) the order of the instructions stays as it is", so nothing changes there: wrong by 14 us** in the profile. The order stayed, the addresses did not. Of the 9.6 us in U 8.1 are shown to be theirs: 4.7 go with equal starts modulo 64 (align), 3.4 more when the left pools lie where they lay (px_const). The 4.7 of the down projection aren't settled: the stretch varied from -8.5 to +6.3 us against before among kernels, also between two with the same layout (gate_sp -2.4, pool_lo +6.3); its cause was not followed.
- **The sum.** 24.7 + 9.6 - 5.1 - 9.6 is 19.6 us; with the smaller stretches of the table (+2.3, -1.9, +4.7) the profile shows 14.5 off, and the median 31. The 11 us between the profiled execution and the median have no trace, and stay open. In the profiled one the clock granted from 410 to 1060 us was 0.94, in the kernel before 0.96.

The fastest version found is align_both, 0.9831 of the kernel before, with px_const level at 0.9836.
